# Second layer of a hybrid encoder: rotary sine products in two operations a token tile, and one query head's probabilities turned in blocks of 32 by VectorE and transfers

## The chip, the core and the metric

One core of a Trainium2 chip runs the whole program. The metric is the device time of one execution in microseconds (us). The time before is the median of three runs. The engines are named as in the profile: PE (TensorE), PEld (its weight loads), DVE (VectorE), ACT (ScalarE), POOL (GpSimd) and SP (SyncE, which issues most transfers).

## The reference, cut to what matters

Two layers over 256 tokens of width 2048. The first mixes tokens with neighbourhood attention, the second, in which the change lies, with grouped-query attention: 12 query heads and 4 key and value heads of width 128, queries and keys normalised by head and turned by rotary positions. Beside them run 4 heads of cross-attention into 256 memory tokens; an output projection and an MLP with squared ReLU follow.

```python
def _rotate(x, ang):
    x1, x2 = jnp.split(x, 2, axis=-1)
    c, s = jnp.cos(ang), jnp.sin(ang)
    return jnp.concatenate([x1 * c - x2 * s, x2 * c + x1 * s], axis=-1)

def axial_rope(x):
    ...
    out = jnp.concatenate([_rotate(xf[..., :half], ang_r),
                           _rotate(xf[..., half:], ang_c)], axis=-1)
...
        z = n @ b_w_in[j]
        q, k, v, qm = jnp.split(z, [MIX_WIDTH, MIX_WIDTH + KV_WIDTH, MIX_WIDTH + 2 * KV_WIDTH], axis=-1)
        q = axial_rope(rms_norm(split_heads(q, N_MIX_HEADS), b_q_norm[j]))
        k = axial_rope(rms_norm(split_heads(k, N_KV_HEADS), b_k_norm[j]))
        mix = gqa_block_attention(q, k, split_heads(v, N_KV_HEADS))
    ...
    h = h + jnp.concatenate([mix, cross], axis=-1) @ w_o[i]
```

All is float32. A head is 128 wide and falls into halves (row and column positions) of 64, each of two quarters of 32 that `_rotate` exchanges.

## The kernel before

**Products.** A float32 operand is split into a high part (an ACT copy, rounded) and a low part (a DVE subtraction), `split` (L516, L517). A product is then three products on PE: high by high, high by low, low by high. In `m_products` (L396, L399, L400) activations of 128 tokens are the stationary operand and 512 columns of weights move. Weights come in chunks of 1 MB over SP's queue (`raw`, three rooms), are split by half chunk into `hi` and `lo` (four rooms each) and used by half chunk: 12 products of `m_products`.

**Order.** A half chunk of weights is a grain, and each grain is followed by a tick. Work other than the weights' products is put in by `later(n, ...)`, n ticks ahead. This gives the program's order. The order in which each engine then gets its instructions is drawn up by a planner that simulates a timeline of its own (`schedule_with_timeline_sim=True`), so that instructions of several ticks may stand mixed on an engine; an engine carries out its list in order.

**The second layer's attention.** The projection is made in blocks of 512 columns: memory queries, keys, values, and then three query blocks (0, 1, 2) of four heads each. The output projection (`add_o`) follows at once, so its products run beside the attention of the last blocks. When a block of keys or queries is summed, `normed_heads` (L1744) takes each of the two token tiles from PSUM: squares and scaling on ACT, a root on POOL, and `turned_by`: a DVE product with the cosines over all of 128x512 (L1749), DVE products with the sines whose input has the quarters exchanged (L1755), and their sum (L1757). There are four blocks of this kind (keys and three of queries), so eight token tiles.

**One head.** `attention` lays a head's steps on ticks. `attend` makes the scores in PSUM (L612 to L614), and `softmaxed` the probabilities `sc` in SBUF: maximum (L570), exponential on ACT (L572), reciprocal (L575) and scaling (L577) on DVE. The product with the values needs them transposed, as `pT`, high and low parts. There are two ways:

- `attend2` (L624): four transposes of 128x128 on PE into the PSUM bank `pt_a`, and a split from there.
- `turned` (L678, L683): two DVE transposes in blocks of 32 into `sc_t`, which takes a second of the three rooms that `sc` has, four transfers on SP's queue that put the blocks in place in `pT_t`, and, ticks later, `halved`, a split from SBUF.

`attend3` (L708 to L710) then makes the six products `av` with the values and splits the result into the head's column of `cat`, which the output projection reads. With four numbers in `steps` a head goes through `turned` and `halved`, with three through `attend2`. Query block 0 (heads 0 to 3) has four, block 2 (heads 8 to 11) three, and block 1 (heads 4 to 7) is parted: heads 4, 5 and 6 have three, head 7 four. The memory heads and the first layer's heads are turned by DVE and transfers too.

Of the kernel before, what the change touches and what calls it, by code (L numbers as in the profile page):

```python
# [14 lines left out]
ALU = mybir.AluOpType  # L15
AX = mybir.AxisListType

P = 128
# [146 lines left out]
def encoder_kernel(ctx: ExitStack, tc: tile.TileContext, t: dict, out: bass.AP):  # L165
    nc = tc.nc
# [208 lines left out]
    def later(n, fn, *args):  # L375
        pending.append((state["tick"] + n, fn, args))
# [142 lines left out]
    def rstd_of(ss, n, name):  # L519

        w = ss.shape[-1]
        v = small.tile([P, w], F32, tag="rs_v", name=f"{name}_v")
        nc.vector.tensor_scalar(v, ss, 1.0 / n, EPS, op0=ALU.mult, op1=ALU.add)
        r = small.tile([P, w], F32, tag="rs_r", name=f"{name}_r")
        nc.gpsimd.tensor_tensor(r, v, mhalf[:, :w], op=ALU.pow)
        return r
# [75 lines left out]
    def attend(qT, kT, bias=None):  # L602
        kT = kT if bias is not None or isinstance(kT, Far) else Near(kT)
        if bias is not None:
            return attend_near(qT, kT, bias)
        sc_ps = at.att.tile([P, NT, SEQ], F32, tag="att", bufs=at.banks, name="sc_ps")
        for s in range(NT):
            i = NT - 1 - s
            qh, ql = qT[:, i * P : (i + 1) * P], qT[:, SEQ + i * P : SEQ + (i + 1) * P]
            kh, kl = kT.part(0), kT.part(1)  # L610
            ps = kT.out(sc_ps[:, s, :])
            nc.tensor.matmul(ps, qh, kh, start=True, stop=False)  # L612
            nc.tensor.matmul(ps, qh, kl, start=False, stop=False)  # L613
            nc.tensor.matmul(ps, ql, kh, start=False, stop=True)  # L614
        sc = at.work.tile([P, NT, SEQ], F32, tag="sc", bufs=3, name="sc")
        softmaxed(sc, sc_ps)
        return sc

    def attend2(sc):
        pt = at.att.tile([P, NT, SEQ], F32, tag="att", bufs=at.banks, name="pt_a")  # L620
        for s in range(NT):
            i = NT - 1 - s
            for k in range(NT):
                nc.tensor.transpose(pt[:, k, i * P : (i + 1) * P], sc[:, s, k * P : (k + 1) * P], ident)  # L624
        pT = at.work.tile([P, 2, NT, SEQ], F32R, tag="pT", bufs=2 + box["layer"], name="pT")
        return pT, split(pT[:, 0], pT[:, 1], pt)
# [43 lines left out]
    def turned(sc):  # L670

        if len(sc.shape) == 2:
            return turned_near(sc)

        blocks = at.work.tile([P, 4, NT, NT, 32], F32, tag="sc", bufs=3, name="sc_t")
        for s in range(NT):

            nc.vector.transpose(blocks[:, :, :, NT - 1 - s, :].rearrange("p b k j -> p k b j"),  # L678
                                sc[:, s, :].rearrange("p (k i b) -> p k b i", k=NT, b=4))
        pT = at.work.tile([P, 2, 4, NT, NT * 32], F32R, tag="pT", bufs=2 + box["layer"], name="pT_t")  # L680
        raw = pT[:, 1].bitcast(F32)
        for a in range(4):
            nc.sync.dma_start(raw[:, a].rearrange("p k c -> p (k c)"),  # L683
                              blocks[a * 32 : (a + 1) * 32].rearrange("p b k t j -> p (b k t j)"))
        return pT

    def halved(pT):

        hi, lo = (pT[:, n, 32:352] if len(pT.shape) == 3 else pT[:, n] for n in range(2))
        return pT, split(hi, lo, lo.bitcast(F32))  # L690
# [31 lines left out]
    def attention(jobs, at, gap=1, steps=(0, 1, 3, 4), rest=0):  # L722


        def step(n, job, prev):
            qT, kT, bias, v, head, cat = job
            if n == 0:
                res = attend(qT, kT, bias)
                box["scaled", head] = box["scaled"]
            elif n == 1 and len(steps) == 4:  # L730
                res = turned(prev)
            elif n < len(steps) - 1:
                res, box["pT", head] = halved(prev) if len(steps) == 4 else attend2(prev)
            else:
                if "between" not in box:
                    return attend3(prev, v, head, cat)
                with tc.issue_after(box.pop("between").ins):
                    return attend3(prev, v, head, cat)
            results[n, head] = res

        results = {}
        for t in range(len(jobs) + len(steps) - 1):
            for n in range(len(steps)):
                if 0 <= t - n < len(jobs):
                    j = t - n
                    more = rest if n == len(steps) - 1 and j == len(jobs) - 1 else 0
                    later(at + gap * j + steps[n] + more,
                          lambda n=n, job=jobs[j]: step(n, job, results.get((n - 1, job[4]))))
# [20 lines left out]
    def head_of(v, hd):  # L769
        return lambda part, kt: v[:, part, kt, hd * HD : (hd + 1) * HD]  # L770
# [973 lines left out]
    def normed_heads(w, wait=False):  # L1744
        cg, sg = box["rope"]
        outs = []

        def turned_by(y, y2, o, i):
            nc.vector.tensor_tensor(o, y, cg[:, i, None, :].to_broadcast([P, 4, HD]), op=ALU.mult)  # L1749
            yv = y.rearrange("p h (a b c) -> p h a b c", a=2, b=2)  # L1750
            y2v = y2.rearrange("p h (a b c) -> p h a b c", a=2, b=2)
            sv = sg[:, i, :].rearrange("p (a b c) -> p a b c", a=2, b=2)
            for a in range(2):
                for b in range(2):
                    nc.vector.tensor_tensor(y2v[:, :, a, b, :], yv[:, :, a, 1 - b, :],  # L1755
                                            sv[:, None, a, b, :].to_broadcast([P, 4, 32]), op=ALU.mult)
            nc.vector.tensor_tensor(o, o, y2, op=ALU.add)  # L1757

        for i in range(NT):
            y2 = at.work.tile([P, 4, HD], F32, tag="b_y2", name="b_y2")  # L1760
            ss = small.tile([P, 4], F32, tag="b_ss", name="b_ss")
            for j in range(4):
                nc.scalar.activation(y2[:, j, :], w.ps[i][:, j * HD : (j + 1) * HD], AF.Square,
                                     scale=box["rstd"][:, i : i + 1], accum_out=ss[:, j : j + 1])
            r = rstd_of(ss, HD, "b_r")
            nc.gpsimd.tensor_scalar(r, r, box["rstd"][:, i : i + 1], None, op0=ALU.mult)
            y = at.work.tile([P, 4, HD], F32, tag="b_y", name="b_y")
            for j in range(4):
                nc.scalar.activation(y[:, j, :], w.ps[i][:, j * HD : (j + 1) * HD], AF.Copy, scale=r[:, j : j + 1])
            o = at.work.tile([P, 4, HD], F32, tag="b_o", bufs=2, name="b_o")  # L1770
            if i and wait:
                with tc.issue_after(box["shares"][-3].ins):
                    turned_by(y, y2, o, i)
            else:
                turned_by(y, y2, o, i)
            outs.append(o.rearrange("p a b -> p (a b)"))
        return outs
# [13 lines left out]
    def b_q_done(blk):  # L1791
        def f(w):
            outs = normed_heads(w, blk == 2)
            qT = at.work.tile([P, 4, 512], F32R, tag="l4", name="qT1")
            if blk == 0:
                later(1, queries_far, outs)
                later(3, queries_split, qT)
            elif blk in (2,):
                later(1, queries_aside, outs)
                later(1, queries_beside, qT)  # L1800
            else:
                later(1, heads_T, outs, 4, qT)
            kvs = [(blk * 4 + j) // (NH // NKV) for j in range(4)]
            jobs = [(qT[:, j, :], Far(box["kT"], kv), None, head_of(box["vb"], kv), blk * 4 + j, box["cat"])
                    for j, kv in enumerate(kvs)]
            if blk == 1:
                attention(jobs[:3], 1, 2, (0, 3, 6))
                attention(jobs[3:], 7, 2, (0, 2, 5, 6))
            else:
                attention(jobs, 1 if blk else 3, 2, (0, 3, 6) if blk else (0, 2, 5, 6), 2 if blk == 2 else 0)  # L1810
        return f
# [205 lines left out]
```

## Time and profile before

| what | us |
|---|---|
| median of three runs | 1988.13 |
| lowest and highest run | 1988.09, 1989.83 |
| the profiled execution's own time | 1988.52 |
| its span, first to last instruction | 1986.6 |
| PE busy in the span | 1976.8 |
| DVE busy | 1744.0 |
| ACT busy | 1451.0 |
| POOL busy | 156.1 |

Busy times are those of one profiled execution. Durations of matrix products overlap, since they are pipelined: what a product holds PE for is read from its start to the start of the next. Idle time of an engine counts only where the end of the program hangs on it. A row of a tile or a line gives the count (x), shortest, median and longest duration in ns, and the first and last start in us; a row in order of time gives start and length in us, and in brackets the idle time before it and what ended it.

### The profile page before, as it was taken

What the parts mean: (1) busy time and instruction counts of PE and PEld (TensorE: products, weight loads), DVE (VectorE), ACT (ScalarE), POOL (GpSimd) and SP (SyncE); (2) the same over time, 40 slices, a digit from 0 to 9 for tenths busy, and PEclk for the clock granted to TensorE, in tenths of its full rate; (3) what the DMA queues carried; (4) which work ended last, traced back from release to release, by engine and by line L of the source; (5) the groups of instructions that cost most, each with busy time, mean ns of one, the idle gap of its engine ahead of it and who ended that gap; (6) DMA issues with size and microseconds to landing.
All of it is one profiled execution on the core that took longest, in us unless ns stands there. A gap on an engine that the chain in (4) does not pass through costs nothing.

```text
span 1986.6 us, 33222 instructions
## 1 busy us (share of the span) xinstructions
PE 1976.8 (100%) x12852; PEld 1797.3 (90%) x12852; DVE 1744.0 (88%) x2132; ACT 1451.0 (73%) x2123; POOL 156.1 (8%) x209
## 2 busy tenths in 40 slices
PE   9999999999999999999999999999999999999998
PEld 8999999899999999999998888889999999999997
DVE  6777768799999999999999879789999999999997
ACT  6655555677887778777887666667788777877786
POOL 0000000000000000000001001001000000000001
PEclk9999999999999999999999999999999999999999
DMA  7856566777777777777778765668777777777775
GB/s 291 321 192 208 203 199 195 273 225 239 228 225 237 230 226 237 233 240 227 223 228 226 268 219 172 221 205 257 238 228 225 236 231 227 236 232 240 229 225 157
DMA packets 113950, 454.57 MB, mean 229 GB/s; under 512 B 19072, under 2 KB 43776, under 8 KB 66432
## 3 DMA queue, kind: packets, MB, share of 16 engines
q1 hardware_dynamic: 92320, 414.43, 61.0%
q0 software_dynamic: 21184, 37.50, 10.8%
q8 instruction: 101, 1.65, 0.3%
q10 hardware_dynamic: 288, 0.52, 0.1%
q14 instruction: 57, 0.47, 0.1%
HBM read 397.78 MB, written 4.19 MB: 202 GB/s over the span
## 4 chain that ended last, share of the span: by engine, by line
PE 98%; ACT 1%; DVE 1%; issue 0%; DMA 0%; SPq 0%; POOL 0%; DVEq 0%; POOLq 0%; ACTq 0%
PE ps_u L419 35%; PE p L1380 10%; PE p L1384 10%; PE p L1383 10%; PE ps_s L419 9%; PE ps_m L399 7%; PE ps_m L400 7%; PE ps_m L396 7%; DMA raw<-in_w_first 0%; PE sc_ps L612 0%; PE sc_ps L614 0%; PE sc_ps L613 0%; PE av L708 0%; PE av L709 0%; PE av L710 0%
## 5 line engine op out<-in xcount | busy, mean ns | idle before, releaser
L419 PE MATMUL ps_u<-hT,uh 128*128 128x256 f32 x3812 | 662.5, 276 | 0.0
L419 PEld LDWEIGHTS ps_u<-hT,uh 128*128 128x128 f32 x3812 | 578.7, 188 | 5.7
L419 PE MATMUL ps_u<-hT,ul 128*128 128x256 f32 x1964 | 542.6, 276 | 0.0
L516 ACT ACTIVATE uh<-raw_U 128x1024 fp32r<-128x1024 f32 x258 | 273.4, 1061 | 157.0 <-PE ps_u L419 155.0
L419 PEld LDWEIGHTS ps_u<-hT,ul 128*128 128x128 f32 x1964 | 368.7, 188 | 0.0
L516 ACT ACTIVATE hi<-raw 128x1024 fp32r<-128x1024 f32 (+2 forms) x215 | 221.0, 1032 | 161.3 <-PE ps_m L400 78.3
L517 DVE TENSOR_TENSOR lo<-raw,hi 128x1024 fp32r<-128x1024 f32 (+2 forms) x215 | 253.4, 1185 | 86.6 <-ACT hi L516 86.1
L517 DVE TENSOR_TENSOR ul<-raw_U,uh 128x1024 fp32r<-128x1024 f32 x258 | 314.1, 1219 | 11.6 <-ACT uh L516 11.6
L517 DVE TENSOR_TENSOR tl<-t,th 128x2048 fp32r<-128x2048 f32 x120 | 274.7, 2290 | 51.7 <-ACT th L516 51.3
L516 ACT ACTIVATE th<-t 128x2048 fp32r<-128x2048 f32 x120 | 230.9, 1924 | 92.5 <-PE p L1384 92.5
L517 DVE TENSOR_TENSOR bl<-b,bh 128x1536 fp32r<-128x1536 f32 x120 | 210.2, 1752 | 0.3 <-ACT bh L516 0.3
L1348 POOL DMA_DIRECT2D t<-b x120 | 103.4, 862 | 1175.6 <-ACT t L1347 1090.6
L1380 PE MATMUL p<-th,a_s 128*128 128x512 f32 x480 | 187.5, 391 | 0.0
L1383 PE MATMUL p<-tl,a_s 128*128 128x512 f32 x480 | 187.2, 390 | 0.0
L1384 PE MATMUL p<-th,a_s 128*128 128x512 f32 x480 | 186.7, 389 | 0.0
L516 ACT ACTIVATE bh<-b 128x1536 fp32r<-128x1536 f32 x120 | 178.7, 1489 | 3.5
L419 PE MATMUL ps_s<-nT,hi 128*128 128x256 f32 x896 | 154.6, 277 | 0.0
L1384 PE MATMUL p<-bh,a_s 128*128 128x512 f32 x360 | 140.9, 391 | 0.0
L1383 PE MATMUL p<-bl,a_s 128*128 128x512 f32 x360 | 140.1, 389 | 0.0
L1380 PE MATMUL p<-bh,a_s 128*128 128x512 f32 x360 | 140.1, 389 | 0.0
L419 PEld LDWEIGHTS ps_s<-nT,hi 128*128 128x128 f32 x896 | 135.3, 188 | 0.2
L419 PE MATMUL ps_s<-nT,lo 128*128 128x256 f32 x448 | 124.2, 277 | 0.0
(343 smaller groups left out, 3715.4 us busy)
## 6 DMA issues: line engine op xcount, KB each, us to landing
raw_U<-in_w_up SPq DMA_DIRECT2D x128, 1024.0 KB, 6.4
b<-in_w_pair SPq DMA_DIRECT2D x120, 1024.0 KB, 5.8
raw<-in_w_o SPq DMA_DIRECT2D x32, 1024.0 KB, 5.0
t<-b POOLq DMA_DIRECT2D x120, 256.0 KB, 6.6
raw<-in_w_b SPq DMA_DIRECT2D x21, 1024.0 KB, 5.6
raw<-in_w_av SPq DMA_DIRECT2D x12, 1024.0 KB, 5.0
raw<-in_w_aq SPq DMA_DIRECT2D x12, 1024.0 KB, 5.0
raw<-in_w_ak SPq DMA_DIRECT2D x12, 1024.0 KB, 4.9
```

Of the source, the lines that this page charges most:

```text
L396: first = nc.tensor.matmul(ps, ah, hi[:, s], start=st, stop=False)
L399: nc.tensor.matmul(ps, ah, lo[:, s], start=False, stop=False)
L400: final = nc.tensor.matmul(ps, al, hi[:, s], start=False, stop=sp)
L419: ins = nc.tensor.matmul(ps, x, acts[:, k, part], start=k == n == 0, stop=k == KT - 1 and n == 2)
L516: first = nc.scalar.activation(dst_hi, src, AF.Copy)
L517: return first, nc.vector.tensor_tensor(dst_lo, src, dst_hi.bitcast(F32), op=ALU.subtract)
L1348: nc.gpsimd.dma_start(s[:, 3, :], b[:, 1, :], accum_op=ALU.add)
L1380: ins = nc.tensor.matmul(ps, a[:, 0, ai, :], hi[:, s], start=entered, stop=False, skip_group_check=True)
L1383: nc.tensor.matmul(ps, a[:, 0, ai, :], lo[:, s], start=False, stop=False, skip_group_check=True)
L1384: nc.tensor.matmul(ps, a[:, 1, ai, :], hi[:, s], start=False, stop=ends, skip_group_check=True)
```

## The change

Two edits. In `turned_by` the four sine products of a token tile, one for each quarter (128 partitions, 4 heads of 32), become two, one for each parity of the quarter (4 heads, 2 halves of 32), with the same elements in all. In `b_q_done` head 4, the first of query block 1, gets four steps for three: its scores still come at tick 1 and its product with the values at tick 7 after the block; between them stand `turned` at tick 3 and `halved` at tick 6 where `attend2` stood at tick 4. Heads 5 and 6 keep their ticks (their first is 3, as it was), and so does head 7.

```diff
-            for a in range(2):
-                for b in range(2):
-                    nc.vector.tensor_tensor(y2v[:, :, a, b, :], yv[:, :, a, 1 - b, :],
-                                            sv[:, None, a, b, :].to_broadcast([P, 4, 32]), op=ALU.mult)
+            for b in range(2):
+                nc.vector.tensor_tensor(y2v[:, :, :, b, :], yv[:, :, :, 1 - b, :],
+                                        sv[:, None, :, b, :].to_broadcast([P, 4, 2, 32]), op=ALU.mult)
...
             if blk == 1:
-                attention(jobs[:3], 1, 2, (0, 3, 6))
+                attention(jobs[:1], 1, 2, (0, 2, 5, 6))
+                attention(jobs[1:3], 3, 2, (0, 3, 6))
                 attention(jobs[3:], 7, 2, (0, 2, 5, 6))
```

## The prediction

> **What bounds the kernel now.** I read the page first: the span, the busy shares, and the chain that ended last.
>
> ```profile
> span 1986.6 us, 33222 instructions
> PE 1976.8 (100%) x12852; PEld 1797.3 (90%) x12852; DVE 1744.0 (88%) x2132; ACT 1451.0 (73%) x2123; POOL 156.1 (8%) x209
> PE 98%; ACT 1%; DVE 1%; issue 0%; DMA 0%; SPq 0%; POOL 0%; DVEq 0%; POOLq 0%; ACTq 0%
> ```
>
> TensorE (PE) holds 98% of the chain. A busy PE need not be a fast one, so next come the busy times by stretch (us: stretch, PE, PEld, DVE, ACT, POOL, then clock, DMA share, GB/s), and all that PE ever waited for.
>
> ```profile
> 20.00:1978.00 1958.00, 1957.91 (x12717) 1779.20 (x12716) 1726.75 (x2097) 1433.66 (x2088) 155.09 (x202) 1.00 0.72 228
> 1220.00:1240.00 20.00, 20.00 (x111) 17.38 (x110) 19.68 (x37) 14.05 (x31) 1.25 (x3) 1.00 0.55 176
> 1240.00:1260.00 20.00, 20.00 (x119) 17.54 (x118) 17.44 (x35) 12.64 (x30) 4.42 (x8) 1.00 0.45 145
> 1970.00:1990.00 20.00, 8.42 (x49) 7.28 (x47) 9.53 (x21) 5.08 (x14) 1.30 (x2) 0.83 0.28 106
> PE idle L245 <- POOL mhalf L239: 1.0, 1, 1.0
> PE ps_s L419 <- ACT hi L516: 0.5, 1, 0.5
> ```
>
> From 20 to 1978 us PE is idle for 0.09 us in all, at full clock; its 1.5 us of waits lie in the first 20 us, and what is left ends in the tail after 1978. So in the second layer's attention, which lies around 1190 to 1275, the end moves only by what leaves PE or by what makes PE wait. VectorE (DVE) is nearly full there, 19.68 of 20 us from 1220 to 1240: no bound of its own, but it has little room for a delay.
>
> **The transposes leave PE.** Head 4 loses the four transposes of `attend2`. The profile's rows: all of that kind, and then those of head 6 in order of time.
>
> ```profile
> L624 PE MATMUL pt_a<-ident,sc x28: 270/272/273, 1232.3 to 1268.7; 128*128 128x128 f32 x28
> 1243.84 0.39 PE L399 MATMUL ps_m<-lo,cat 128*128 128x512 f32 x1
> 1244.06 0.60 PE L624 MATMUL pt_a<-ident,sc 128*128 128x128 f32 x4
> 1244.42 0.36 PE L708 MATMUL av<-pT,vb 128*128 128x256 f32 x1
> 1244.62 0.28 PE L709 MATMUL av<-pT,vb 128*128 128x256 f32 x1
> 1244.74 0.28 PE L710 MATMUL av<-pT,vb 128*128 128x256 f32 x1
> ```
>
> One transpose is reported with 272 ns, but they overlap: the four start at 1244.06 and the next product at 1244.42, so they hold PE for 0.36 us. That product then keeps 0.20 us to its follower (1244.42 to 1244.62), where its like keep 0.12 (1244.62 to 1244.74), so 0.08 more goes with the change of kind. Price on PE: 0.36 + 0.08 = 0.44 us. The bounds are four bare steps of 0.09 (0.36) and four full durations, 4 x 0.272 = 1.09; I take 0.44, since it is read from start to start and holds all that the products behind lose. This is on the path: -0.44 us.
>
> TensorE: Matmul & The Clock Gate, Part 4: PE-mode transpose, in the Trainium skill, gives about 275 ns for a 128x128 transpose inside a kernel. As a duration the trace agrees (272 ns); as a cost it does not, for the steps are 0.09 us. By the page the sum would be -1.1 us, a time near 1987.0.
>
> **What takes their place.** Head 4 now goes the way of heads 0 to 3 and 7: two DVE transposes in blocks of 32, four transfers issued on SP, and a split out of SBUF. The rows of the five heads of this layer's mixer that go that way, and those of the seven that go over PE:
>
> ```profile
> L678 DVE STREAM_TRANSPOSE sc_t<-sc x10: 587/614/649, 1203.9 to 1245.7; 128x256 f32<-128x256 f32 x10
> L683 SPq DMA_DIRECT2D pT_t<-sc_t x20: 543/595/606, 1205.1 to 1248.3; - x20
> DMA to landing us min/median/max: 2.1/2.2/4.8
> L516 ACT ACTIVATE pT_t<-pT_t x5: 632/632/634, 1210.6 to 1250.6; 128x512 fp32r<-128x512 f32 x5
> L517 DVE TENSOR_TENSOR pT_t<-pT_t x5: 647/684/692, 1211.7 to 1251.8; 128x512 fp32r<-128x512 f32 x5
> L516 ACT ACTIVATE pT<-pt_a x7: 593/599/606, 1233.8 to 1269.1; 128x512 fp32r<-128x512 f32 x7
> L517 DVE TENSOR_TENSOR pT<-pt_a,pT x7: 639/681/692, 1237.0 to 1269.7; 128x512 fp32r<-128x512 f32 x7
> ```
>
> DVE gains 2 x 0.614 = 1.2 us (1.1 when the two run back to back), and its split costs the same 0.68. ScalarE (ACT) gains 0.632 - 0.599 = 0.03. SP issues four transfers more, 4 x 0.595 = 2.4 us of its queue, 64 KB each, which land 2.2 us after. POOL issues nothing for it. One of the four PSUM banks of the attention is asked for once less, and one of the three score rooms ("sc") once more. None of this is PE's work: on the path it costs nothing as long as head 4's probabilities are there when PE comes to them. That cover is to be read from the steps in time: heads 0 and 3 on the new way, head 4 on the old one.
>
> ```profile
> 1203.89 1.16 DVE L678 STREAM_TRANSPOSE sc_t<-sc 128x256 f32<-128x256 f32 x2
> 1211.73 0.65 DVE L517 TENSOR_TENSOR pT_t<-pT_t 128x512 fp32r<-128x512 f32 x1
> 1213.98 0.28 PE L708 MATMUL av<-pT_t,vb 128*128 128x256 f32 x1
> 1226.74 1.13 DVE L678 STREAM_TRANSPOSE sc_t<-sc 128x256 f32<-128x256 f32 x2
> 1234.37 0.68 DVE L517 TENSOR_TENSOR pT_t<-pT_t 128x512 fp32r<-128x512 f32 x1
> 1230.04 1.14 DVE L577 TENSOR_SCALAR sc<-sc,rs 128x256 f32<-128x256 f32 x4
> 1237.04 1.27 DVE L517 TENSOR_TENSOR pT<-pt_a,pT 128x512 fp32r<-128x512 f32 x2
> 1240.78 0.28 PE L708 MATMUL av<-pT,vb 128*128 128x256 f32 x1
> ```
>
> From the first block transpose to the end of the split head 0 took 1203.89 to 1212.38, 8.5 us, and head 3 1226.74 to 1235.05, 8.3 us. Head 4's shares are scaled by 1231.2 (with head 5's). 1231.2 + 8.5 = 1239.7, and PE's product with head 4 comes at 1240.78: 1.1 us in hand, in an order of PE that was drawn up for the old way (there the split was done by about 1237.7, so 3.1 us in hand). The new order on every engine comes from a planner's own estimates, which I cannot see; but with those estimates the thinnest lead of the heads shown is head 0's, 1212.38 to 1213.98, 1.6 us, and no turned head ever made PE wait. I take 0 for the wait. It cannot be below zero, since PE has only 0.09 us to give back; its upper bound is worked out under the rivals.
>
> The weight splits and loads are the other work that stands behind the new instructions, in DVE's order and in SP's. Waits from 1100 to 1330 (us, times, longest), those of SP's queue from 1180 to 1290, and SP's row there:
>
> ```profile
> ACT hi L516 <- PE ps_m L400: 35.4, 27, 1.7
> DVE sc_t L678 <- DMA pT_t<-sc_t: 2.0, 2, 1.3
> SPq L279 <- DVE lo L517: 55.4, 11, 17.5
> 1230.52 4.29 SPq L279 DMA_DIRECT2D raw<-in_w_o  x2
> ```
>
> ACT's splits wait 27 times for PE to free one of the four split rooms: the weights run ahead of PE, not behind it. And SP stands idle for most of the time until DVE's subtraction frees a chunk's room; 2.4 us of issues fit in there. So: nothing on the path.
>
> **The sine products.** Eight token tiles (keys, and three query blocks, two each) have four DVE products of 128x128 and get two of 128x256.
>
> ```profile
> L1755 DVE TENSOR_TENSOR b_y<-b_y,sin_q x24: 281/284/290, 1173.0 to 1231.3; 128x128 f32<-128x128 f32 x24
> 1196.42 0.89 DVE L1755 TENSOR_TENSOR b_y<-b_y,sin_q 128x128 f32<-128x128 f32 x4
> L517 DVE TENSOR_TENSOR cat<-av,cat x12: 405/416/426, 1218.3 to 1273.1; 128x256 fp32r<-128x256 f32 x12
> L1749 DVE TENSOR_TENSOR b_o<-b_y,cos_q x6: 672/683/692, 1172.4 to 1229.0; 128x512 f32<-128x512 f32 x6
> ```
>
> Four products back to back take 0.89 us. Two of 128x256 are not shown with these operands; they cannot well be cheaper than one product over all 512 elements (0.68), and at worst the third stride costs as much as it saves (0.89). By the nearest row, 0.416 each, less the 0.08 that neighbours overlap (4 x 0.284 - 0.89 = 0.25 over three joints), two take 0.75. So 0.14 us less a tile, 0.28 a block, 1.1 us in all, on DVE alone: with PE full throughout, 0 on the path. Beside head 4's 1.1 us it makes DVE's balance about +0.3 us around blocks 1 and 2 (1.1 - 3 x 0.28).
>
> **Sum.** -0.44 + 0 + 0 = -0.44 us. The profiled execution took 1988.52 us (span 1986.6 and 1.9 around it), 0.39 above the median of three, 1988.13: it becomes 1988.08, and the median 1987.69. A measurement of this kernel tells a change from none from about 0.2% on, 4 us; this is a ninth of that.
>
> **The rivals.** (a) Head 4 comes late, and PE waits at its product. For: only 1.1 us in hand at the old place, and DVE's transposes have waited for score rooms (1.3 us at the longest). With the slowest landing of the row, 4.8 for 2.2 us, the split is done at 1239.7 + 2.6 = 1242.3, and PE stands 1.5 us; with a wait for a room on top, 2.8. Less the 0.44 that is +1.1 to +2.4: 1989.2 to 1990.5. Against: leads of the turned heads so far.
>
> (b) The transposes free their full durations, -1.09: 1987.0. Against: their starts.
>
> (c) Slower by more than 4 us: DVE's delay empties the weight rooms. Place: 1231 to 1245, where DVE is full; the block transposes (1.1) wait for a score room (1.3), and the splits of weights and heads behind them slide by 2.4. PE uses a half chunk in 12 products of 0.23 us, 2.7 us, and with four rooms and the waits above two halves, 5.4 us, lie ready. It decides only if the slide grows past 5.4, by SP's queue standing behind `turned` and the loads landing late as well; at a slide of 10 us PE loses 4.6, a time of 1992.3. Against: a slide of 2.4, and ACT's 27 waits for PE.
>
> In VectorE: DVE Perf Modes, Rules for kernel authors, the Trainium skill sends a 128x128 transpose to TensorE where PSUM will do as its target. Taken alone that speaks against the change; the trace has the PE way at 0.44 us of a full engine and the other at 1.1 us of one that waits, so by the rows it binds only if (a) or (c) does.
>
> (d) Nothing goes: the planner's new order breaks up heads 5 and 6 into more changes of kind, 0.08 each, and eats the 0.44: 1988.1.
>
> **How the numbers follow.** The forecast 0.65; (a) 0.19; (b) 0.03; (c) 0.06; (d) 0.05; 0.02 stays for a gain of over 4 us, for which no row has room. Same: 0.65 + 0.19 + 0.03 + 0.05 = 0.92; slower 0.06; faster 0.02. The time is the likeliest's, 1987.7. The range runs from (b) on the lowest run, 1988.09 - 1.09 = 1987.0, to the upper end of (a), 1990.5; the highest run before less 0.44, 1989.4, lies inside.
>
> **What would show it.** 28 transposes `pt_a` become 24, and `sc_t` has 12 block transposes and 24 issues in this layer's mixer heads; PE from 20 to 1978 is still idle for about 0.1 us, and its last product ends 0.4 us sooner; L1755's successor shows 16 products of about 0.42 us, and DVE's busy time changes by no more than a microsecond; between the end of head 4's split and its product there is a lead of a microsecond or more. I am wrong if PE shows a wait for `pT_t`, `cat` or `lo` between 1190 and 1290, or if a step on PE there stretches beyond the 0.23 or 0.12 us that its kind has.

## The result and the profile after

The changed kernel takes 1994.11 us in the median of its runs (1992.40 to 1995.46); the kernel before took 1988.92 us beside it (1988.09 to 1990.35). The ratio is 1.0024, 95% interval [1.0015, 1.0034]: 5.2 us slower. The forecast was 1987.7, the range ended at 1990.5, and slower by over 0.2% had 6 in 100: the prediction was wrong, in sign and in size.

The profiled execution of the changed kernel took 1992.40 us, 3.9 more than the 1988.52 of before. Its page (span, busy times, chain):

```profile
span 1990.5 us, 33214 instructions
PE 1976.9 (99%) x12848; PEld 1796.4 (90%) x12848; DVE 1744.1 (88%) x2118; ACT 1449.9 (73%) x2123; POOL 156.4 (8%) x209
PE 94%; DVE 2%; ACT 1%; DMA 1%; issue 1%; SPq 0%; DVEq 0%; POOL 0%; POOLq 0%; ACTq 0%
```

No engine has more work: four products fewer on PE, DVE busy for 1744.1 after 1744.0. Yet the chain has left PE: 94% for 98%. The time must have gone into waits of PE, and one stretch by windows, before and then after, shows where (the first figure behind the stretch is its length, the second PE's busy time).

```profile
1190.00:1290.00 100.00, 100.00 (x528) 85.95 (x527) 84.35 (x152) 66.91 (x159) 11.50 (x16) 1.00 0.57 197
```

```profile
1190.00:1290.00 100.00, 95.68 (x503) 81.47 (x503) 82.49 (x144) 64.07 (x157) 11.88 (x16) 1.00 0.54 182
```

PE idles for 4.3 us in the second layer's attention, where it never idled before. Three products wait there; in PE's rows in order of time the idle time and what ended it stand in brackets:

```profile
1239.09 0.39 PE L708 MATMUL av<-pT_t,vb 128*128 128x256 f32 x1 [0.48 <-ACT pT_t L516]
...
1246.00 0.36 PE L708 MATMUL av<-pT,vb 128*128 128x256 f32 x1 [1.39 <-DVE cat L517]
...
1255.75 0.38 PE L612 MATMUL sc_ps<-kT,qT 128*128 128x256 f32 x1 [2.45 <-ACT qT L516]
```

The first is head 4's own product, the one that the change hands to the slower way. The second is head 5's, which waits for the PSUM bank that DVE's `cat` empties. The third, the longest, are the scores of head 8, in the next query block, which the change does not touch. The rows of all the score products of these heads, before and after:

```profile
L614 PE MATMUL sc_ps<-kT,qT x24: 281/282/369, 1192.2 to 1262.9; 128*128 128x256 f32 x24
```

```profile
L614 PE MATMUL sc_ps<-kT,qT x24: 279/282/293, 1191.8 to 1267.1; 128*128 128x256 f32 x24
```

The first starts 0.4 us sooner (a shorter start-up, which no part of the change touches), the last 4.2 later. For a stretch with the same products in it but for the four transposes, I take the first score product's start (L612, 1191.38 before and 1190.97 after) to the start of the MLP's first product (L419, 1320.52 and 1324.79): 129.1 us before and 133.8 after, 4.7 more. The terms come to 4.6: 4.3 of idle time; 0.6 for the last products before the three pauses, whose ends no follower overlaps (the one before the third counts 0.39 us, where its like are followed after 0.23); 0.2 for the first products after a pause (1239.09 to 1239.32, 0.23 for 0.12); less the 0.44 of the transposes.

**From head 4 to head 8.** The chain of cause runs through ACT's and DVE's orders. ACT, before and after: the first exponentials (L572) of head 5 and, after, of head 6, and the split of head 4.

```profile
1227.91 0.48 ACT L572 ACTIVATE sc<-sc_ps,nm 128x256 f32<-128x256 f32 x1 [1.65 <-DVE sc_t L678]
```

```profile
1232.22 0.47 ACT L572 ACTIVATE sc<-sc_ps,nm 128x256 f32<-128x256 f32 x1 [0.75 <-DVE sc_t L678]
...
1233.59 0.47 ACT L572 ACTIVATE sc<-sc_ps,nm 128x256 f32<-128x256 f32 x1 [0.35 <-DMA pT_t<-sc_t]
...
1238.41 0.63 ACT L516 ACTIVATE pT_t<-pT_t 128x512 fp32r<-128x512 f32 x1 [2.33 <-DMA pT_t<-sc_t]
```

The exponential writes into one of the three score rooms. Now `sc` of head 4, `sc_t` of head 3 and `sc_t` of head 4 hold all three, so head 5 waits until DVE has turned head 4 and its first room is free: 4.3 us later than before, and head 6 waits for the transfers of head 3. ACT then stands 2.33 us for head 4's transfers. DVE in the same stretch, before (one row; the two splits ahead of it stand in the prediction) and after:

```profile
1238.23 2.09 DVE L1731 STREAM_TRANSPOSE b_y_h<-b_o 128x512 f32<-128x512 f32 x2
```

```profile
1231.03 1.15 DVE L678 STREAM_TRANSPOSE sc_t<-sc 128x256 f32<-128x256 f32 x2
...
1233.95 0.75 DVE L1754 TENSOR_TENSOR b_y<-b_y,sin_q 128x256 f32<-128x256 f32 x2
...
1239.07 0.69 DVE L517 TENSOR_TENSOR pT_t<-pT_t 128x512 fp32r<-128x512 f32 x1 [0.92 <-ACT pT_t L516]
...
1242.30 0.68 DVE L517 TENSOR_TENSOR pT<-pt_a,pT 128x512 fp32r<-128x512 f32 x1
1242.90 2.05 DVE L1731 STREAM_TRANSPOSE b_y_h<-b_o 128x512 f32<-128x512 f32 x2
...
1245.45 0.74 DVE L517 TENSOR_TENSOR cat<-av,cat 128x256 fp32r<-128x256 f32 x2
```

L1731 is a piece of the kernel that the prediction never named. The queries of block 2 are turned in blocks of 32 as well, and their transposes are held back by hand until head 5's split has been issued:

```python
            with tc.issue_after(box["pT", 5][1].ins):      # head 5's low part, L517
                nc.vector.transpose(blocks..., src[i]...)  # L1731
            for a in range(4):
                nc.gpsimd.dma_start(raw[...], blocks[...])  # L1734
```

So head 5's split at 1242.30 (in a pair from 1237.04 before) lets these transposes start at 1242.90 for 1238.23, 4.7 us late. Behind them in DVE's order stand the maximum of head 7's scores and the `cat` subtractions that empty head 5's bank, and POOL's eight transfers wait for them. (A second gate of this kind, L1772 in the kernel before, holds the rotation of block 2's second token tile behind head 5's reciprocal. It slid from 1229.05 to 1233.36, but the rotation was still done well before 1242.90.)

The last link to PE is ACT's order. Here are the second split of the queries (`qT`) and the split of head 7 (`pT_t`), before and then after:

```profile
1248.82 0.62 ACT L516 ACTIVATE qT<-b_y_h 128x512 fp32r<-128x512 f32 x1
...
1250.56 0.63 ACT L516 ACTIVATE pT_t<-pT_t 128x512 fp32r<-128x512 f32 x1
```

```profile
1253.60 0.63 ACT L516 ACTIVATE pT_t<-pT_t 128x512 fp32r<-128x512 f32 x1 [1.42 <-DMA pT_t<-sc_t]
1254.14 1.04 ACT L516 ACTIVATE hi<-raw 128x1024 fp32r<-128x1024 f32 x1
1255.09 0.61 ACT L516 ACTIVATE qT<-b_y_h 128x512 fp32r<-128x512 f32 x1
```

And PE's product of head 8 in the kernel before, which reads the high part that this split of ACT makes (the low part, from DVE, is read only by L614, at 1252.79 at the earliest):

```profile
1251.60 0.28 PE L612 MATMUL sc_ps<-kT,qT 128*128 128x256 f32 x1
```

Before, the split ended at 1249.44, 2.2 us ahead of the product. After, it comes 6.3 us later, and PE is ready for it (1253.30, where its work before the pause ends) 1.7 us later: 6.3 - 2.2 - 1.7 = 2.4, the wait. The queries' own transfers do not set this time. POOL started the last of them at 1248.4 and the longest took 3.0 us, so all had landed by about 1251.4, 3.7 us ahead of the split. What the split stood behind was head 7's split, which waited 1.42 us for head 7's transfers, and a weights' split. Before, it stood ahead of head 7's. So the late gate reaches PE by way of head 7, whose maximum it delays, and of an order on ACT that the planner drew anew.

### The profile page after: what moved, and what is told of

It is laid out like the page before. It is cut to its first block, busy times and chain, and to the rows that moved or that the text cites. A ratio compares the mean times of both kernels' runs of the same rounds, so it can differ in the third digit from the quotient of the medians.

```text
span 1990.5 us, 33214 instructions
## 1 busy us (share of the span) xinstructions
PE 1976.9 (99%) x12848; PEld 1796.4 (90%) x12848; DVE 1744.1 (88%) x2118; ACT 1449.9 (73%) x2123; POOL 156.4 (8%) x209
## 3 DMA queue, kind: packets, MB, share of 16 engines
q8 instruction: 101, 1.65, 0.3%
## 4 chain that ended last, share of the span: by engine, by line
PE 94%; DVE 2%; ACT 1%; DMA 1%; issue 1%; SPq 0%; DVEq 0%; POOL 0%; POOLq 0%; ACTq 0%
PE ps_u L419 35%; PE p L1380 10%; PE p L1384 10%; PE p L1383 10%; PE ps_s L419 9%; PE ps_m L399 6%; PE ps_m L400 6%; PE ps_m L396 6%; DMA pT_t<-sc_t 1%; DVE lo L517 0%; ACT hi L516 0%; SPq L683 0%; DVE sc_t L678 0%; DMA raw<-in_w_first 0%; ACT sq L868 0%
## 5 line engine op out<-in xcount | busy, mean ns | idle before, releaser
L419 PE MATMUL ps_u<-hT,uh 128*128 128x256 f32 x3812 | 662.5, 276 | 0.0
L419 PEld LDWEIGHTS ps_u<-hT,uh 128*128 128x128 f32 x3812 | 578.6, 188 | 5.7
L419 PE MATMUL ps_u<-hT,ul 128*128 128x256 f32 x1964 | 542.6, 276 | 0.0
L419 PEld LDWEIGHTS ps_u<-hT,ul 128*128 128x128 f32 x1964 | 368.6, 188 | 0.0
L419 PE MATMUL ps_s<-nT,hi 128*128 128x256 f32 x896 | 154.6, 277 | 0.0
L419 PEld LDWEIGHTS ps_s<-nT,hi 128*128 128x128 f32 x896 | 135.4, 188 | 0.2
L419 PE MATMUL ps_s<-nT,lo 128*128 128x256 f32 x448 | 124.2, 277 | 0.0
```

Source lines behind the costliest of these rows:

```text
L419: ins = nc.tensor.matmul(ps, x, acts[:, k, part], start=k == n == 0, stop=k == KT - 1 and n == 2)
```

## The experiments

Each is an edit of the kernel before or of the changed one. The start of the queries' block transposes (L1731) and PE's idle time from 1190 to 1290 are from the profiled execution, the medians and ratios from all runs, each against the kernel before on the same chip.

| kernel | L1731 us | PE idle us | median us (before) | ratio [95%] |
|---|---|---|---|---|
| before | 1238.23 | 0.00 | | |
| changed | 1242.90 | 4.32 | 1994.11 (1988.92) | 1.0024 [1.0015, 1.0034] |
| sine_alone | 1240.28 | 1.14 | 1990.62 (1989.01) | 1.0010 [1.0001, 1.0019] |
| turn_alone | 1246.54 | 5.43 | 1996.02 (1989.01) | 1.0038 [1.0026, 1.0051] |
| rooms_4 | 1241.22 | 1.56 | 1989.84 (1989.01) | 1.0005 [0.9996, 1.0014] |
| gate_head_4 | 1240.26 | 1.65 | 1990.18 (1989.01) | 1.0006 [0.9997, 1.0015] |
| before_gate_head_6 | 1246.28 | 3.13 | 1994.06 (1988.99) | 1.0024 [1.0015, 1.0034] |
| sine_gate_head_4 | 1239.60 | 0.38 | 1990.40 (1988.99) | 1.0007 [0.9998, 1.0016] |
| rooms_4_gate_head_4 | 1241.80 | 2.08 | 1989.15 (1988.99) | 0.9999 [0.9990, 1.0009] |
| before_spare_work | 1239.82 | 0.43 | 1989.68 (1988.99) | 1.0005 [0.9996, 1.0013] |
| rooms_5 | 1241.75 | 1.31 | 1990.08 (1988.74) | 1.0008 [0.9999, 1.0017] |
| before_rooms_5 | 1238.97 | 0.73 | 1990.33 (1988.74) | 1.0008 [0.9999, 1.0016] |
| rooms_5_late_product | 1239.63 | 0.06 | 1988.62 (1988.74) | 0.9999 [0.9989, 1.0008] |
| after_again | 1243.45 | 4.88 | 1993.98 (1988.66) | 1.0027 [1.0017, 1.0036] |

One thing runs through all fourteen profiled executions. In six of them (changed, after_again, turn_alone, before_gate_head_6, rooms_4, rooms_5) ACT's order has head 7's split ahead of the queries' second split, and these are the six in which PE waits at head 8's scores: 2.45, 2.47, 3.13, 3.13, 0.45 and 1.31 us. In the other eight the queries' split stands ahead, and PE has no such wait. The start of L1731 does not sort them by itself: rooms_4_gate_head_4, at 1241.80, has no such wait, and rooms_4, at 1241.22, has one. No run changed this order alone, so it is not shown how far a late start makes the planner choose it.

**sine_alone** and **turn_alone**: the kernel before with the first edit of the diff only, and with the second only.

> The kernel before with the two sine products alone; head 4 stays on TensorE. Three theories. Rooms: head 4's second score room makes head 5's softmax wait for head 4's block transposes, and with it everything that is ordered behind head 5's split. Work: the added DVE transposes and SP issues are too much for a stretch in which DVE is full. Order: any edit here makes the planner draw up a worse order. Rooms and work: no change, ratio 0.999 to 1.001, no PE step stretched by more than 0.3 us between 1190 and 1290. Order: slower, by 1 us or more, ratio over 1.0005.

> The kernel before with head 4 turned by VectorE and transfers alone; the sine products stay four. Rooms: about as slow as the whole change, ratio 1.002 to 1.003, with head 5's first exponential at 1231 or later (1227.9 before) and PE waits of 3.5 us or more in sum between 1235 and 1260. Work: slower than the whole change by up to 1 us more, since DVE has 1.1 us more to do. Order: anything between before and after.

sine_alone came out as the third theory, a new order, had it (ratio 1.0010, over the 1.0005 named for it), but only just: two operations fewer a tile cost 1.6 us, at the limit of what can be told from none. turn_alone (1.0038) lies above what any of the three had, though the marks named for the room came: head 5's first exponential at 1231.77, and 5.4 us of waits. DVE's order in sine_alone, ahead of the queries' transposes:

```profile
1238.15 0.69 DVE L517 TENSOR_TENSOR pT<-pt_a,pT 128x512 fp32r<-128x512 f32 x1
1238.75 0.68 DVE L570 TENSOR_REDUCE nm<-sc_ps 128x2 f32<-128x512 f32 x1
1239.35 0.42 DVE L517 TENSOR_TENSOR cat<-av,cat 128x256 fp32r<-128x256 f32 x1
1239.68 0.68 DVE L517 TENSOR_TENSOR pT<-pt_a,pT 128x512 fp32r<-128x512 f32 x1
1240.28 2.10 DVE L1731 STREAM_TRANSPOSE b_y_h<-b_o 128x512 f32<-128x512 f32 x2
```

In the order before, the splits of heads 4 and 5 stood side by side. In the planner's new order head 4's split itself comes 1.1 us later, a maximum and a `cat` subtraction stand between the two, and the gate passes the delay on: 2.05 us. ACT then stands for the queries' transfers with weight splits behind it, and PE for those (ACT's row, then PE's waits):

```profile
1249.41 0.63 ACT L516 ACTIVATE qT<-b_y_h 128x512 fp32r<-128x512 f32 x1 [2.19 <-DMA b_y_h<-b_y_h]
1249.95 1.99 ACT L516 ACTIVATE hi<-raw 128x1024 fp32r<-128x1024 f32 x2
```

```profile
PE ps_m L396 <- ACT hi L516: 0.6, 1, 0.6
PE ps_m L399 <- DVE lo L517: 0.5, 1, 0.5
```

The turn alone costs 7.0 us by the medians, more than the whole change (five runs, and the intervals of the two ratios overlap): the same chain, longer, with the queries' transposes at 1246.54. PE's three longest waits there:

```profile
PE sc_ps L612 <- ACT qT L516: 3.1, 1, 3.1
PE av L708 <- ACT pT_t L516: 1.0, 1, 1.0
PE ps_m L399 <- DVE lo L517: 0.9, 1, 0.9
```

By the medians the parts do not add up (1.6 and 7.0; together 5.2). That fits orders drawn up anew for each edit, but the intervals are too wide to show it.

**rooms_4** and **gate_head_4**: the changed kernel with a fourth score room, and with the gate moved to head 4's split.

```diff
-tag="sc", bufs=3     # in all five places
+tag="sc", bufs=4
```

```diff
-            with tc.issue_after(box["pT", 5][1].ins):
+            with tc.issue_after(box["pT", 4][1].ins):
```

> The whole change with four score rooms for three (every tile of that tag), all else as it was. Rooms: head 5's first exponential comes back to about 1228, its split to 1239 or sooner, the PE waits of 1.6 and 2.6 us are gone, head 4's own wait of 0.65 us may stay: ratio to the kernel before 0.9995 to 1.0007. Work: DVE and SP have the same to do, so 2 us or more of PE waits stay, ratio over 1.001. Order: another order, anything between.

> The whole change, but the block transposes of the third query block's queries (queries_aside) are ordered on DVE after head 4's split instead of after head 5's. Head 5's softmax stays late. Rooms: the wait of 2.6 us for the queries (scores of head 8) goes, since those transposes come 3 us sooner; the waits of 0.65 us at head 4's product and of 1.6 us at head 5's stay: about 2.5 us faster than the whole change, ratio to the kernel before 1.0008 to 1.0017. Work: the same work in the same stretch, so the wait only moves, ratio 1.002 or more. Order: no forecast.

Each by itself takes back most of the loss (ratios 1.0005 and 1.0006, both intervals hold 1); the second gains more than was expected of it. With four rooms head 5's exponential is back at 1227.38, and the next room wait shows up one head later, in ACT's order:

```profile
1227.38 0.47 ACT L572 ACTIVATE sc<-sc_ps,nm 128x256 f32<-128x256 f32 x1 [0.68 <-DVE sc_t L678]
...
1233.14 0.48 ACT L572 ACTIVATE sc<-sc_ps,nm 128x256 f32<-128x256 f32 x1 [4.73 <-DMA pT_t<-sc_t]
```

With the gate on head 4 the queries' transposes start at 1240.26 and the wait at head 8 is gone; what is left of PE's waits are the products of heads 4 and 5 and the transposes of head 6:

```profile
PE av L708 <- ACT pT_t L516: 0.7, 1, 0.7
PE pt_a L624 <- DVE pT L517: 0.5, 1, 0.5
PE av L708 <- DVE cat L517: 0.4, 1, 0.4
```

**before_gate_head_6** is the reverse test: the kernel before, head 4 still on PE, four sine products, and only the gate moved back by one head (`box["pT", 6]`). **sine_gate_head_4** is sine_alone with the gate on head 4, and **rooms_4_gate_head_4** the changed kernel with both mends.

> The kernel before, with the block transposes of the third query block's queries ordered on DVE after head 6's split instead of head 5's, and nothing else. Late queries (the theory after the first four runs: what costs time is that these transposes come later than at 1238; each later start showed more PE waits, 1240.3: 1.4 to 2.4 us, 1242.9: 4.9, 1246.5: 7.3): they start at about 1246, PE waits 5 to 8 us between 1240 and 1262, ratio to the kernel before 1.0025 to 1.004. Head 4's own cost (score room, DVE and SP work) as the cause by itself: no change, since head 4 stays on TensorE, ratio under 1.001.

> The two sine products alone, with those block transposes ordered after head 4's split. Late queries: they start 1.7 us sooner than in the run with the sine products alone (1240.3), at about 1238.5 as in the kernel before; the waits for weights (0.75 and 0.69 us) go, ratio 0.9995 to 1.0004. Order as such (any new order costs): 1.0005 or more stays.

> The whole change with four score rooms and those block transposes ordered after head 4's split: does it beat the kernel before? Late queries: they start before 1241; the wait of 0.6 us for head 8's scores goes, head 4's own wait (0.65 to 1.3 us at its product with the values) stays, against 0.44 us of transposes gone: ratio 1.0000 to 1.0005, no gain. If head 4's lateness is also a matter of the order, ratio under 1.0000.

Moving the gate suffices: without either edit of the change, it gives 1.0024, the whole change's ratio. The test is stronger than the case, though: it moves the transposes by 8.0 us, where the change moved them by 4.7, and PE waits 3.1 us, where 5 to 8 were expected. By the rows of the transfers (the last started at 1251.8, the longest 2.4 us) and a split of 0.6 us, about 1.0 of the 3.1 would be left if the queries' split stood ahead of head 7's on ACT; this is an estimate. PE's wait, and the windows after it (the figure before the last two is the granted clock):

```profile
PE sc_ps L612 <- ACT qT L516: 3.1, 1, 3.1
```

```profile
1257.00:1260.00 3.00, 3.00 (x18) 3.00 (x19) 1.72 (x4) 0.38 (x1) 0.00 (x0) 0.69 0.50 210
1260.00:1262.00 2.00, 2.00 (x8) 1.62 (x7) 1.57 (x5) 1.84 (x8) 0.00 (x0) 0.61 0.00 0
```

The clock adds to the wait: PE's products step by 0.21 us for 0.12 and by 0.43 for 0.23 there, 1.5 us more in all. With 0.3 at the edges of the pause that is 4.9 us, which is what the stretch from the first score product to the MLP takes more here (134.0 us for 129.1). sine_gate_head_4 is inconclusive: the two weight waits are gone and 0.38 us of idle time is left there, but its ratio, 1.0007, is not to be told from sine_alone's 1.0010 nor from 1; its profiled execution holds another 1.1 us wait in the first layer (L591, for the keys). That wait comes and goes between executions of one kernel (none in the first profiled execution of the changed kernel, 0.4 us in the second), and it is 1.4 to 1.5 us in those of sine_alone, before_gate_head_6 and rooms_5_late_product, too. rooms_4_gate_head_4 ties with before (0.9999), with the queries' transposes at 1241.80 where they were expected before 1241. Its profiled execution is the slowest of its runs, so its idle time, a wait of 2.08 us at head 4's product, is not typical.

**before_spare_work** asks whether it is the work alone that costs. The kernel before, with head 4's two block transposes and four transfers done in addition, into rooms of their own:

```diff
             if blk == 1:
+                later(3, lambda: spare(box["sc", 4]))   # 2 transposes, 4 transfers on SP
...
                 attention(jobs[:3], 1, 2, (0, 3, 6))
```

> The kernel before, and as additional work at tick 3 head 4's two block transposes and four SP transfers into two rooms of their own, whose result nobody reads (head 4 itself still goes over TensorE). It is the change's work without its score room and without PE's dependence on it. Score room as the main cause: the queries' block transposes start by 1239.5 (1.1 us later at most), PE waits under 1 us, ratio under 1.0007. Work as the main cause: start at 1241 or later, PE waits 2 us or more, ratio over 1.001.

0.7 us by the medians, not to be told from nothing. The queries' transposes slide by 1.59 us (1238.23 to 1239.82, between the bounds named for the two theories), and PE waits once, 0.43 us for a weight's low part. So DVE's and SP's time by itself does not make the 5.2 us.

**rooms_5**, **before_rooms_5** and **rooms_5_late_product**: the changed kernel with five rooms, the kernel before with five, and the changed one with five, the gate on head 4 and head 4's product one tick later (`(0, 2, 5, 7)` for `(0, 2, 5, 6)`).

> The whole change with five score rooms. With four the wait for a room had only gone on to head 6 (ACT stood 4.7 us before its first exponential, ahead of both splits of heads 3 and 4 in ACT's order). Score room as the cause of the late queries: ACT's wait for head 6's room is under 1.5 us, the queries' block transposes start before 1240.5, PE waits no more than 1.5 us in all between 1230 and 1262, head 4's own among them; ratio 0.9995 to 1.0004. DVE's and SP's work as the cause: as with four rooms or worse, start at 1241 or later, ratio 1.0005 or more.

> The kernel before with five score rooms and nothing else: what the rooms do by themselves. PE had no wait to give back, so at best no change, 0.9997 to 1.0003; if any new order costs something, 1.0003 to 1.001 with waits of PE between 1190 and 1290 of 0.5 to 2 us.

> Meant to beat both: the whole change with five score rooms, head 4's product with the values one tick (some 2.7 us) later (steps 0, 2, 5, 7), and the queries' block transposes ordered after head 4's split. Late queries and late head 4 as the two causes: no PE wait over 0.3 us between 1190 and 1290, so only the 0.44 us of the transposes is left, ratio 0.9994 to 1.0000. Otherwise a wait is left that this account does not have, ratio over 1.0003.

With five rooms no exponential waits for one, and still the queries' transposes come at 1241.75, 3.5 us late. By the bounds set beforehand the score room as the cause of the late queries failed here: start and ratio (1.0008) are those named for the work. ACT's row in rooms_5 shows another reason, the waiting for what SP transfers:

```profile
1238.21 0.63 ACT L516 ACTIVATE pT_t<-pT_t 128x512 fp32r<-128x512 f32 x1 [2.85 <-DMA pT_t<-sc_t]
1238.75 1.05 ACT L516 ACTIVATE hi<-raw 128x1024 fp32r<-128x1024 f32 x1
1239.70 0.58 ACT L516 ACTIVATE pT<-pt_a 128x512 fp32r<-128x512 f32 x1
```

ACT stands for head 4's transfers, and head 5's split is two places behind. The room is one part of the delay, head 4's transfers in ACT's order another. How much each has in the changed kernel can't be read off, since every edit also draws a new order: five rooms in the kernel before, where PE waited for nothing, gave 0.73 us of idle time and a ratio of 1.0008, whose interval holds 1. With room, gate and tick mended together PE idles for 0.06 us from 1190 to 1290, as before, and the time ties: 0.9999 [0.9989, 1.0008]. It beats the changed kernel and is not shown to beat the one before. The 0.44 us of the transposes do not show even in its profiled execution: from the first score product to the MLP it takes 129.37 us, before 129.14. What else holds PE longer there was not traced.

**after_again**: the changed kernel, unedited.

> The changed kernel once more, unedited. Its profiled execution took 1992.40 us, the lowest of its nine, 1.7 below their median of 1994.11; the question is where those 1.7 us lie in the other executions. Clock theory: PE's wait of about 2.5 us at the scores of head 8 is followed, in most executions, by some 3 us at a granted clock of 0.5 to 0.7 (turn_alone had 0.50 to 0.60 after a wait of 3.1, before_gate_head_6 had 0.61 to 0.69). A profiled execution of 1994 to 1995.5 us then shows PE's idle time between 1190 and 1290 within 0.7 us of the 4.3 seen before, and a stretch of clock under 0.8 there in which products of 0.23 us step by 0.43. Rival, late transfers: the clock stays at 1.00 there, and the idle time between 1190 and 1290 is 6 us, 1.7 more than 4.3, with the surplus behind waits that end at a transfer (pT_t or b_y_h). Should the profiled execution be one of the quick ones, near 1992.4, this tells neither. The median by both: 1993.5 to 1994.7, ratio 1.0018 to 1.0032.

This profiled execution was one of the quicker ones again, 1992.97 us, and tells neither. It repeats the waits for `qT` (2.5) and `cat` (1.4); head 4's is 1.0 for 0.5.

Its runs and the nine of the changed kernel, 19 in all, say a little more: ten have a mean granted clock of 0.999 and 1993.3 us on average, nine one of 0.998 or 0.997 and 1994.7. All runs of rooms_4, gate_head_4 and rooms_5_late_product, where PE's longest wait in this attention is 1.1 us, have 0.999. That fits a clock that falls after the wait at head 8 in about half of the executions. It is no proof: the kernel before, where PE has no wait in this attention, shows 0.998 too, in 12 of its 97 runs beside the experiments, and no such execution of the changed kernel was profiled: the 1.0 to 1.7 us between its profiled executions and its median stay open.

## Why the prediction was wrong

**The step that failed** is "What takes their place", which ended in "I take 0 for the wait". The waits were 4.3 us. It failed in four places.

- A score room "once more" was priced by the longest wait that a row of before showed, 1.3 us on DVE, and only for head 4. The room is taken from head 5: its exponential came 4.3 us later, on ACT. The row of before that carried the warning is the 1.65 us that head 5's exponential already waited for `sc_t` of head 3; it was not among the rows quoted.
- Head 4's lead was taken against PE's old order. The forecast of the data was right: the split was to end at 1239.7, and it ended at 1239.76 (1239.07 + 0.69). But PE came to head 4's product at 1238.61, 2.2 us sooner than the 1240.78 that the prediction used, and found not even the high part there.
- The lead was read for head 4's product alone. Who else waits for what stands behind the new waits was asked for weights, and not for head 7 and the next block's queries, which a gate holds behind head 5's split. This gave the largest wait, 2.45 us. gate_head_4, in which it is gone, shows that moving the gate takes it away; that the order of two splits on ACT carries it is read from the traces.
- The planner's new order was counted as harmless (rival (d) gave it 0.44 us at most). It moved head 7's split ahead of the queries' on ACT and head 4's product forward on PE. The sine products alone cost 1.6 us by the medians, and five rooms in the kernel before 1.6; the first interval only just excludes no change, the second holds it.

**Rival (a)**, head 4 late, came true with 0.48 us of idle time where it had 1.5 to 2.8: the mechanism was there, as the smallest of the three waits. **Rival (c)** had the sign: DVE's order slides and something behind it runs out. But it looked for weights, and decided from a slide of 5.4 us; in the changed kernel it was a bank and the queries, with 4.7 us. Weight waits showed in sine_alone, turn_alone and others, up to 0.9 us each, and none in the changed kernel. The stated sign of being wrong, a wait for `pT_t` or `cat` between 1190 and 1290, came; the longest wait, for `qT`, was not among the signs. One size in the prediction is also off: DVE's balance around blocks 1 and 2 takes off three blocks' savings where two lie there (1.1 - 2 x 0.28 = +0.5). Nothing hangs on it.

**What held.** PE lost its four transposes, and their price closes the sum of the changed kernel above. With the waits taken away (rooms_5_late_product) PE is as full as before between 1190 and 1290. The sine pair takes 0.75 us, as forecast, and the tiles of the changed kernel have the counts:

```profile
L683 SPq DMA_DIRECT2D pT_t<-sc_t x24: 542/596/626, 1204.4 to 1251.4; - x24
L678 DVE STREAM_TRANSPOSE sc_t<-sc x12: 587/632/649, 1203.2 to 1248.8; 128x256 f32<-128x256 f32 x12
...
L1754 DVE TENSOR_TENSOR b_y<-b_y,sin_q x12: 417/419/426, 1172.5 to 1234.3; 128x256 f32<-128x256 f32 x12
L1754 DVE TENSOR_TENSOR b_y<-b_y,sin_k x4: 422/424/424, 1128.8 to 1130.4; 128x256 f32<-128x256 f32 x4
```

DVE's busy time changed by 0.1 us. The Trainium skill's advice in VectorE: DVE Perf Modes, Rules for kernel authors, to take a 128x128 transpose to TensorE where PSUM will do, was set aside because the rows had it as the dearer way for the full engine. Here the trace agrees with the advice: turn_alone is slower, with a ratio of 1.0038 [1.0026, 1.0051]. By the rows above, though, what costs here is no engine's busy time but the room that the other way takes and ACT's standing for its transfers (2.33 us in the changed kernel).

## What to carry to other kernels

A step that takes one more buffer of a shared ring can delay the next user of the ring more than itself: find that user in the trace of before, see what it already waits for, and follow its followers through every engine's order until a lead is larger than the delay. A lead read from the old order holds only as long as both ends keep their places: head 4's data came when it was forecast, and PE asked for it 2.2 us sooner. Orderings written by hand (`issue_after` and the like) carry a delay from one head to a block that the change doesn't touch, so list them before pricing an edit as hidden. Where a planner draws the orders, an edit on a side engine is not free by its work alone: here two such edits left PE idle for 1.1 and 0.7 us in their profiled executions, where the sine products shrank and where rooms were only added.

## What the hardware showed that was not expected

A wait of PE can cost more than its length. In turn_alone the wait of 3.13 us at head 8's scores was followed by windows at a granted clock of 0.5 to 0.6, and in rooms_4_gate_head_4 one of 2.08 us at head 4's product was, too. The windows of both runs:

```profile
1260.00:1262.00 2.00, 2.00 (x12) 2.00 (x11) 0.43 (x2) 0.38 (x1) 0.00 (x0) 0.50 0.00 0
1262.00:1265.00 3.00, 3.00 (x11) 2.52 (x11) 2.44 (x7) 1.93 (x8) 0.00 (x0) 0.60 0.00 0
```

```profile
1242.00:1245.00 3.00, 3.00 (x13) 2.58 (x12) 3.00 (x4) 0.86 (x3) 1.36 (x3) 0.59 0.72 288
```

In turn_alone the clock is 0.50 from the end of the wait, 1258.61, to 1264.32, and PE's products step by 0.21 us for 0.12 and by 0.43 for 0.23: 2.5 us more are lost. With the 5.43 of idle time, some 1.3 at the edges of its five pauses (at 0.26 each, as in the changed kernel) and less the 0.44, that is 8.8; the stretch from the first score product to the MLP takes 138.2 us for 129.1, 9.1 more. In rooms_4_gate_head_4 the clock is 0.50 from 1241.21 to 1244.40. The Trainium skill, TensorE: Matmul & The Clock Gate, Part 1, has the clock at half after an idle window of about 3.4 us, in windows that run free of the program. The half agrees; the length does not, since 2.08 and 3.13 us were enough here. After 2.45 and 2.47 us, in the two profiled executions of the changed kernel, the clock stayed at 1.00. So the length of a wait does not tell by itself whether the clock falls; what does stays open.
